# Seven block products over pairs of feature tiles for the long sequence's gate and up-projection, with the down-projection as a phase of its own

## The chip, the cores and the metric

The kernel runs on one core of one Trainium2 chip. The metric is the device time of one launch in microseconds. One launch computes the whole encoder layer for two sequences that share the weights: a long one of 1024 tokens and a short one of 512 tokens. TensorE (PE) multiplies, VectorE (DVE), ScalarE (ACT) and GpSimd (POOL) do the elementwise work, and SyncE (SP) issues all DMAs from one queue. Each engine runs its own instructions strictly in the order of the program.

## The reference, cut to what matters

Everything is fp32. After the attention part, each sequence goes through the output projection and a gated feed-forward part; the change is in the latter.

```python
def conv_glu_sublayer(x, g_ffn, w_ff_gate, w_ff_up, conv_w, conv_b, w_ff_down):
    n = rms_norm(x, g_ffn)
    gate = n @ w_ff_gate                      # 1024 -> 2816
    pad = jnp.pad(gate, ((0, 0), (1, 1), (0, 0)))
    gate = pad[:, :-2] * conv_w[0] + pad[:, 1:-1] * conv_w[1] + pad[:, 2:] * conv_w[2] + conv_b
    return x + (jax.nn.gelu(gate, approximate=False) * (n @ w_ff_up)) @ w_ff_down
# then: h = rms_norm(h, g_final); the 16 meta tokens in front are dropped
```

The convolution has width 3 over positions, so the gate at the first real token needs the gate at the last meta token too.

## The kernel before, in words

**Precision.** Each fp32 operand is split into two numbers of a type that PE reads in one pass: `hi`, the value cast on ACT (line 102), and `lo`, the rest, subtracted on DVE or POOL (line 103). A product is three matmuls into the same PSUM bank (`mm3`, lines 108 to 110): hi·hi, hi of the weights times lo of the input, lo of the weights times hi of the input.

**Layout.** Features lie on the 128 partitions, tokens along the free dimension. A weight tile (`w_f`, 128x1024, 512 KB) holds eight 128x128 blocks: the columns of one tile of output features, for all eight tiles (`KT`) of the 1024 input features. `load_weight` (lines 121 to 129) loads one and splits it.

**Order of the stages.** The program is written with generators, which `merge` interleaves. First come the two projections and the attentions. The short sequence's output projection and feed-forward part (`f1`) run beside the long sequence's attention and then beside the long sequence's output projection (`mixer_out`, line 772), which works in three chunks of 340 to 344 tokens and keeps its result `h` in SBUF. What is left of `f1` is its last group of down-projections in two halves of 256 tokens, and the final norm with its output stores (`y`, lines 635 to 644). For the short sequence there are two `y` buffers of 128x256 and one buffer for the squares that POOL adds up (line 487).

**The long sequence's feed-forward part** (`conv_glu(0)`, line 778) is the end of the program. It first scales `h` by the norm into `xhi`, `xlo` (lines 559 to 566), chunk by chunk, so that PE starts on the first chunk while the others are made. Then it goes through the 22 tiles of the 2816 features in eleven pairs. For each pair: gate products in three chunks of 342 to 344 tokens, convolution straight from PSUM (lines 585 to 589), Gelu, up products in three chunks, multiplied into the gate (line 603) and split, and then the down-projection of the two tiles at once, in 16 products of 512 tokens, each added to `h` on DVE (line 615). For the last pair the down-projection runs in four chunks of 256 tokens, and the final norm of each follows while the next is multiplied.

**What sets the order.** The framework schedules the instructions of each engine ahead of time, from the dependences, the buffers of the pools and a model of their times. The resulting order is fixed in the program.

## Time and profile before

| | us |
|---|---|
| median of 3 runs (2226.34 to 2230.16) | 2229.71 |
| profiled execution | 2230.43 |
| its span, first to last instruction | 2228.6 |
| PE busy | 2128.2 (95%) |
| DVE busy | 1463.7 (66%) |
| ACT busy | 1069.8 (48%) |
| POOL busy | 812.3 (36%) |
| granted PE clock, mean | 0.98 |

Times of the trace count from the start of the span. A timeline row gives start, duration, engine, line, operation, output <- inputs, shape, and in brackets the idle time before it with what ended it. Matmuls overlap, so the cost of one is the distance from its start to the next one's start, not its duration.

### The profile page before, as it was taken

How to read it: one execution, taken by the hardware profiler on the slowest of the kernel's cores; microseconds unless marked ns; L12 is line 12 of the kernel's file. 1: busy time of each engine (PE TensorE's matmuls, PEld its weight loads, DVE VectorE, ACT ScalarE, POOL GpSimd, SP SyncE). 2: the span in 40 equal slices, each digit the busy share in tenths (PEclk: the TensorE clock that was granted, in tenths of full speed). 3: DMA queues.
4: the chain of work that ended last, by engine and by line, in shares of the span. 5: the costliest groups of instructions: out<-in, count | busy, mean ns of one | idle time of the engine just before them, and what ended most of it. 6: DMA issues, size and time to landing. Idle time of an engine off the chain costs nothing.

```text
span 2228.6 us, 36288 instructions
## 1 busy us (share of the span) xinstructions
PE 2128.2 (95%) x13474; PEld 1984.5 (89%) x13474; DVE 1463.7 (66%) x3453; ACT 1069.8 (48%) x1921; POOL 812.3 (36%) x649
## 2 busy tenths in 40 slices
PE   7999998997999999999999999999999999999997
PEld 6888888996987998898988899989999999999997
DVE  6876787767788777788878865784443344433446
ACT  6534566544567566776776655551222221212224
POOL 3465546864445333355444423431111000111005
PEclk9999999998999999999999999999999999999999
DMA  6555335446321322232322125721111111111112
GB/s 226 163 168 191 113 93 157 166 170 196 101 80 54 101 72 65 72 124 80 121 90 76 65 73 172 221 93 48 48 38 57 48 48 48 48 38 57 48 39 76
DMA packets 113137, 219.80 MB, mean 99 GB/s; under 512 B 13728, under 2 KB 69824, under 8 KB 112448
## 3 DMA queue, kind: packets, MB, share of 16 engines
q1 hardware_dynamic: 112960, 217.48, 30.4%
q8 instruction: 106, 1.74, 0.3%
q14 instruction: 71, 0.58, 0.1%
HBM read 168.93 MB, written 48.50 MB: 98 GB/s over the span
## 4 chain that ended last, share of the span: by engine, by line
PE 76%; DVE 12%; issue 4%; ACT 4%; DMA 3%; POOL 2%; SPq 1%; DVEq 0%; ACTq 0%; POOLq 0%
PE ps_mm L108 18%; PE ps_mm L109 18%; PE ps_mm L110 18%; PE ps_t L370 5%; PE ps_s L347 3%; PE ps_s L348 3%; DVE p L349 2%; DVE w_lo L103 2%; PE ps_o L385 1%; PE ps_o L384 1%; PE ps_s L108 1%; PE ps_s L110 1%; PE ps_s L109 1%; DMA w_f<-w_in 1%; DMA x<-xT 1%
## 5 line engine op out<-in xcount | busy, mean ns | idle before, releaser
L108 PE MATMUL ps_mm<-xhi,w_hi 128*128 128x342 f32 (+6 forms) x2320 | 726.5, 314 | 12.4 <-ACT xhi L177 6.4
L109 PE MATMUL ps_mm<-xlo,w_hi 128*128 128x342 f32 (+6 forms) x2320 | 721.3, 311 | 8.8 <-DVE xlo L103 4.6
L110 PE MATMUL ps_mm<-xhi,w_lo 128*128 128x342 f32 (+6 forms) x2320 | 719.8, 310 | 0.0
L108 PEld LDWEIGHTS ps_mm<-xhi,w_hi 128*128 128x128 f32 x2320 | 441.5, 190 | 20.2 <-ACT xhi L177 7.2
L109 PEld LDWEIGHTS ps_mm<-xlo,w_hi 128*128 128x128 f32 x2320 | 441.6, 190 | 16.3 <-DVE xlo L103 6.8
L110 PEld LDWEIGHTS ps_mm<-xhi,w_lo 128*128 128x128 f32 x2320 | 442.1, 191 | 1.0
L102 ACT CAST w_hi<-w_f 128x1024 fp32r<-128x1024 f32 x200 | 207.5, 1047 | 388.9 <-PE ps_mm L109 341.9
L103 POOL TENSOR_TENSOR a_lo<-gate,a_hi 128x256 fp32r<-128x256 f32 (+2 forms) x110 | 120.4, 1097 | 725.6 <-ACT a_hi L102 725.6
L103 DVE TENSOR_TENSOR w_lo<-w_f,w_hi 128x1024 fp32r<-128x1024 f32 x183 | 264.6, 1453 | 125.9 <-ACT w_hi L102 123.8
L349 DVE TENSOR_SCALAR_CACHE_REDUCE p<-ps_s 114x344 f32<-114x344 f32 (+4 forms) x562 | 257.6, 487 | 41.8 <-PE ps_s L348 23.3
L615 DVE TENSOR_TENSOR h<-ps_mm,h 128x512 f32<-128x512 f32 (+1 forms) x288 | 182.0, 644 | 122.3 <-PE ps_mm L110 121.4
L354 ACT ACTIVATE p<-p,nm 114x1040 f32<-114x1040 f32 (+5 forms) x212 | 215.0, 1014 | 87.3 <-DVE nm L352 84.5
L102 ACT CAST pt_hi<-ps_t 128x512 fp32r<-128x512 f32 (+6 forms) x360 | 168.8, 483 | 154.4 <-PE ps_t L370 132.4
L421 POOL TENSOR_TENSOR p<-p,r 128x1040 f32<-128x1040 f32 (+1 forms) x96 | 159.2, 1666 | 188.0 <-DVE r L356 125.7
L109 PE MATMUL ps_mm<-a_lo,w_hi 128*128 128x512 f32 (+1 forms) x576 | 216.1, 375 | 2.1 <-POOL a_lo L103 2.1
L108 PE MATMUL ps_mm<-a_hi,w_hi 128*128 128x512 f32 (+1 forms) x576 | 213.8, 382 | 2.4 <-DVE h L615 1.6
L110 PE MATMUL ps_mm<-a_hi,w_lo 128*128 128x512 f32 (+1 forms) x576 | 215.7, 374 | 0.0
L103 DVE TENSOR_TENSOR pt_lo<-ps_t,pt_hi 128x512 fp32r<-128x512 f32 (+4 forms) x312 | 171.7, 561 | 50.5 <-ACT pt_hi L102 49.0
L347 PE MATMUL ps_s<-k,q 128*114 128x348 f32 (+4 forms) x552 | 184.3, 338 | 14.3 <-DVE p L349 13.7
L370 PE MATMUL ps_t<-ident,p 128*128 128x128 f32 (+7 forms) x1188 | 183.6, 270 | 2.4 <-DVE pt_lo L103 2.1
L348 PE MATMUL ps_s<-k,q 128*114 128x348 f32 (+4 forms) x552 | 172.8, 318 | 1.3 <-DMA q<-qk 1.3
L370 PEld LDWEIGHTS ps_t<-ident,p 128*128 128x128 f32 (+7 forms) x1188 | 140.9, 136 | 31.6 <-issue 6.8
(158 smaller groups left out, 3638.3 us busy)
## 6 DMA issues: line engine op xcount, KB each, us to landing
w_f<-w_gate SPq DMA_DIRECT2D x44, 512.0 KB, 3.5
w_f<-w_up SPq DMA_DIRECT2D x44, 512.0 KB, 3.5
w_f<-w_down SPq DMA_DIRECT2D x44, 512.0 KB, 3.6
w_f<-w_in SPq DMA_DIRECT2D x36, 512.0 KB, 4.1
w_f<-w_out SPq DMA_DIRECT2D x32, 512.0 KB, 3.6
q<-qk SPq DMA_DIRECT2D x32, 257.0 KB, 3.7
q<-qk SPq DMA_DIRECT2D x48, 171.0 KB, 2.9
qk<-hi SPq DMA_DIRECT2D x42, 192.0 KB, 2.0
```

The costliest lines, as they stand in the source:

```text
L102: nc.scalar.copy(hi, src)
L103: (lo_engine or nc.vector).tensor_tensor(out=lo, in0=src, in1=hi.bitcast(F32), op=ALU.subtract)
L108: nc.tensor.matmul(ps, lhsT=whi, rhs=xhi, start=start, stop=False)
L109: nc.tensor.matmul(ps, lhsT=whi, rhs=xlo, start=False, stop=False)
L110: nc.tensor.matmul(ps, lhsT=wlo, rhs=xhi, start=False, stop=stop)
L347: nc.tensor.matmul(ps, lhsT=q[0], rhs=k[:, c0:c0 + cw], start=True, stop=False)
L348: nc.tensor.matmul(ps, lhsT=q[1], rhs=k[:, c0:c0 + cw], start=False, stop=True)
L349: nc.vector.tensor_scalar(out=p[:, c0:c0 + cw], in0=ps, scalar1=HD ** -0.5, scalar2=-3.0e38, op0=ALU.mult, op1=ALU.max, accum_out=mx[:, i: ...
L354: nc.scalar.activation(p, p, AF.Exp, bias=nm, accum_out=l)
L370: nc.tensor.transpose(tps[:, c:c + M], p[:, k0:k0 + kw], g.ident[:M, :M])
L421: nc.gpsimd.tensor_tensor(out=p, in0=p, in1=r.broadcast_to([P, n]), op=ALU.mult)
L615: nc.vector.tensor_tensor(out=hs, in0=ps, in1=hs, op=ALU.add)
```

## The change

For a pair of feature tiles, the 1024 input features are cut into halves of 512 (four tiles each), and the 1024 real tokens into halves of 512. The pair's weights are then a 2x2 matrix of blocks a11, a12 (first tile), a21, a22 (second tile), the input a 2x2 matrix x11, x12, x21, x22. Eight block products would make the four results. The changed kernel makes them by seven, with sums of weight blocks (s1 to s4, on POOL, anew for each pair) and of input blocks (t1 to t4, once), and combines the products with additions (u2, v, u3). One block product is four tiles times three matmuls of 512 tokens.

- `combine` makes the seven input matrices, each as hi and lo, before the first product.
- The gate at the last meta token is made apart: eight multiply-adds on DVE over 128x128 (`g0`, lines 808 to 810) and one fp32 matmul with a vector of ones (line 813), per tile.
- `winograd` makes the seven products of a pair; weight halves of 512 columns are split with six buffers each for hi and lo (`HB`), with three buffers for whole weights (`WB`) and three for sums (`SB`).
- The products gate·up (`act`) go to DRAM. After all eleven pairs a second phase reads them back and does the down-projection for three chunks of tokens (512, 256, 256): eight PSUM banks, one for each output tile, add up over all 22 feature tiles. So `w_down` is loaded and split three times. The residual `h` is written to DRAM by `mixer_out` and read back at each chunk's end, which is followed by the final norm.

```diff
@@ mixer_out
-                w = load_weight(g, wp, g.w_out[j], bufs=wb)
+                w = load_weight(g, wp, g.w_out[j], bufs=wb) if s == 1 else load_halves(g, wp, g.w_out[j])
...
+                    if s == 0:
+                        nc.sync.dma_start(out=g.h[j, :, c0:c0 + cw], in_=h[:, j, c0:c0 + cw])
@@ new
+def split_half(g, wp, src, lo_engine=None):
+    hi = wp.tile([P, H], F32R, name="w_hi", tag="w_hi", bufs=HB)
+    lo = wp.tile([P, H], F32R, name="w_lo", tag="w_lo", bufs=HB)
+    split(g, hi, lo, src, lo_engine)
+    return hi, lo
...
+def combine(g, st, xp, tp):
...
+    def normed(k, c0):
+        hs = h[:, k, c0:c0 + H]
+        nc.vector.scalar_tensor_tensor(out=hs, in0=hs, scalar=g.gain[:, V_GFFN + k:V_GFFN + k + 1],
+                                       in1=rstd[:, c0:c0 + H], op0=ALU.mult, op1=ALU.mult)
+        return hs
+    def kept(nm, i, src):
+        split(g, x[nm][0][:, i], x[nm][1][:, i], src, nc.gpsimd if i % 2 else nc.vector)
+    def minus(a, b, i):
+        t = tp.tile([P, H], F32, name="x_t", tag="x_t", bufs=4)
+        (nc.vector if i % 2 else nc.gpsimd).tensor_tensor(out=t, in0=a, in1=b, op=ALU.subtract)
+        return t
...
+    for i in range(HT):
+        x11[i], x21[i] = normed(i, 1), normed(HT + i, 1)
+        kept("x11", i, x11[i])
+        kept("x21", i, x21[i])
+    for i in range(HT):
+        x12[i], x22[i] = normed(i, 1 + H), normed(HT + i, 1 + H)
+        t1 = minus(x12[i], x11[i], i)
...
+def winograd(g, wp, up, x, raw):
...
+    s1 = s_(ALU.add, a21, a22)
+    p1 = product(split_half(g, wp, a11), x["x11"])
+    c1 = tile("c1")
+    nc.scalar.copy(c1, p1)
+    yield 0, 0, product(split_half(g, wp, a12), x["x21"]), c1
+    p5 = product(split_half(g, wp, s1), x["t1"])
+    c5 = tile("c5")
+    nc.scalar.copy(c5, p5)
+    s2 = s_(ALU.subtract, s1, a11)
+    u2 = plus("u2", nc.vector, product(split_half(g, wp, s2), x["t2"]), c1)
+    v = plus("v", nc.gpsimd, u2, c5)
+    s3 = s_(ALU.subtract, a11, a21)
+    p7 = product(split_half(g, wp, s3), x["t3"])
+    u3 = plus("u3", nc.vector, p7, u2)
+    yield 1, 1, p7, v
+    s4 = s_(ALU.subtract, a12, s2)
+    yield 0, 1, product(split_half(g, wp, s4), x["x22"]), v
+    yield 1, 0, product(split_half(g, wp, a22), x["t4"]), u3
+def conv_glu_long(ctx, g, st, wp, es_h):
...
+        for i in range(2):
+            acc = up.tile([P, P], F32, name="g0", tag="g0")
...
+            ps = g.psum.tile(P, 2, "mm")
+            nc.tensor.matmul(ps, lhsT=acc, rhs=g.ones2, start=True, stop=True)
+            nc.scalar.copy(gate[:, i, 0:1], ps[:, 0:1])
+        for i, half, ps, rest in winograd(g, wp, up, x, raw):
+            nc.vector.tensor_tensor(out=gate[:, i, 1 + half * H:1 + (half + 1) * H], in0=ps, in1=rest, op=ALU.add)
...
+        for i, half, ps, rest in winograd(g, wp, up, x, raw):
+            a = act[:, i, half * H:(half + 1) * H]
+            t = up.tile([P, H], F32, name="sum", tag="sum")
+            nc.vector.tensor_tensor(out=t, in0=ps, in1=rest, op=ALU.add)
+            nc.gpsimd.tensor_tensor(out=a, in0=t, in1=a, op=ALU.mult)
+        for i in range(2):
+            nc.sync.dma_start(out=g.act[f0 + i], in_=act[:, i])
...
+    for c0, cw in ((0, H), (H, H // 2), (H + H // 2, H // 2)):
+        last = c0 + cw == N
+        ps = [g.psum.tile(P, cw, "mm") for _ in range(KT)]
+        for f in range(NFF):
+            a = op.tile([P, H], F32, name="a_f", tag="a_f", bufs=3)[:, :cw]
+            nc.sync.dma_start(out=a, in_=g.act[f, :, c0:c0 + cw])
+            ahi, alo = (t[:, :cw] for t in split_act(g, wp, a, cw))
+            w = load_halves(g, wp, g.w_down[f])
+            for j in range(KT):
+                mm3(g, ps[j], *block(w, j), ahi, alo, f == 0, f == NFF - 1)
...
+            nc.vector.tensor_tensor(out=h[:, j], in0=ps[j], in1=res, op=ALU.add)
...
+                sq = op.tile([P, H], F32, name="sq", tag="sq", bufs=4)[:, :cw]
+                nc.scalar.activation(sq, h[:, j], AF.Square)
+                nc.gpsimd.tensor_tensor(out=acc, in0=acc, in1=sq, op=ALU.add)
...
+            mean_rsqrt(g, op, rs, acc, cw)
@@ trunk_kernel
-    drain(conv_glu(ctx, g, 0, st0, "left", wp0, 3, 2))
+    drain(conv_glu_long(ctx, g, st0, wp0, es_h))
```

Three places of the order that the framework made, on the engines that wait or are waited for. The numbers behind the names are the program's numbers of the tiles.

PE, from the long sequence's output projection to its feed-forward part, before: `ps_s` is the last tile of the projection, `ones_d` the matmul that sums squares for the norm, `xhi` the scaled input.

```order
L108 MATMUL ps_s_16959<-xhi_16342,w_hi_16952 128x340
L109 MATMUL ps_s_16959<-xlo_16350,w_hi_16952 128x340
L110 MATMUL ps_s_16959<-xhi_16342,w_lo_16953 128x340
L492 MATMUL ps_s_17024<-acc_16358,ones_d_108 128x340
L108 MATMUL ps_mm_19035<-xhi_18916,w_hi_19031 128x344
```

The same place in the change (`a_hi` is the short sequence's activation, in its last down-projections, `g0` the gate at the last meta token):

```order
L112 MATMUL ps_s_17082<-xhi_16426,w_lo_17072 128x340
L110 MATMUL ps_mm_18932<-a_hi_18718,w_hi_18784 128x256
...
L520 MATMUL ps_s_17148<-acc_16442,ones_d_110 128x340
L520 MATMUL ps_mm_18943<-acc_18791,ones_d_110 128x256
L110 MATMUL ps_mm_18977<-a_hi_18654,w_hi_18778 128x256
...
L520 MATMUL ps_mm_18999<-acc_18878,ones_d_110 128x256
L813 MATMUL ps_mm_19193<-ones2_112,g0_19184 128x2
L813 MATMUL ps_mm_19205<-ones2_112,g0_19196 128x2
L110 MATMUL ps_mm_19214<-x11_hi_19050,w_hi_19210 128x512
```

Before, PE went from the norm's sum straight to the first gate product. Now 15 down-projection matmuls and two norm sums of the short sequence, and the two `g0` matmuls, stand between the last output projection and the first block product.

DVE at that place in the change: `y` is the short sequence's output (12 rows of it stand here, two of them shown), `x_t` a sum of input blocks.

```order
L712 SCALAR_TENSOR_TENSOR h_15044<-h_15044,gain_130,rstd_15045 128x512 x8
L645 TENSOR_TENSOR h_6876<-ps_mm_18977,h_6876 128x256
...
L671 SCALAR_TENSOR_TENSOR y_18951<-h_6876,gain_130,rstd_6877 128x256
...
L671 SCALAR_TENSOR_TENSOR y_19026<-h_6876,gain_130,rstd_6877 128x256
L707 SCALAR_TENSOR_TENSOR x0_19064<-h_15044,rstd_15045,gain_130 128x8
L105 TENSOR_TENSOR x11_lo_19051<-h_15044,x11_hi_19050 128x512
...
L721 TENSOR_TENSOR x_t_19166<-h_15044,x_t_19156 128x512
L808 TENSOR_SCALAR g0_19184<-w_f_19180,x0_19064 128x128
L808 TENSOR_SCALAR g0_19196<-w_f_19182,x0_19064 128x128
```

The short sequence's outputs, which before lay among the output projection's instructions, now all stand behind its last row; the input matrices' splits stand behind them, and `g0` behind these. On ACT the first cast of x11 likewise stands behind the last `y`.

PE at the change from the first to the second chunk of the new down phase (22855 is the last of the eight banks of the first chunk, 23819 the first of the second):

```order
L110 MATMUL ps_mm_22855<-w_hi_23698,w_hi_23708 128x512
L111 MATMUL ps_mm_22855<-w_lo_23699,w_hi_23708 128x512
L112 MATMUL ps_mm_22855<-w_hi_23698,w_lo_23709 128x512
L520 MATMUL ps_mm_23785<-acc_23738,ones_d_110 128x512
L110 MATMUL ps_mm_23819<-w_hi_23829,w_hi_23835 128x256
```

The norm's sum over the chunk that has ended stands ahead of the first product of the next one.

More of the change, by code (lines that the diff above doesn't have):

```diff
@@ L23 @@
 KT = D // P
+H = D // 2
+HT = KT // 2
 NMETA = 16
@@ L667, in merge, with split_act @@
+def split_act(g, wp, a, cw):
+    hi = wp.tile([P, H], F32R, name="w_hi", tag="w_hi", bufs=HB)
+    lo = wp.tile([P, H], F32R, name="w_lo", tag="w_lo", bufs=HB)
+    split(g, hi[:, :cw], lo[:, :cw], a)
+    return hi, lo
 def merge(a, wa, b, wb):
@@ L689 @@
 MB = 5
+HB = 6
+WB = 3
+SB = 3
 R1, R2, R3 = (1.0, 0.9), (1.0, 0.4), (1.0, 1.0)
@@ L714, in trunk_kernel @@
     nc.vector.memset(g.ones_d, 1.0 / D)
+    g.ones2 = const.tile([P, 2], F32, name="ones2")
+    nc.vector.memset(g.ones2, 1.0)
     g.ones_v = const.tile([P, P], F32, name="ones_v")
```

123 lines of the change are left out of this document (117 added, 6 removed).

## The prediction

> **What bounds the kernel now.** I read the page's engine shares first, then busy time by stretches, then the timeline of PE where the changed part begins and ends.
>
> ```profile
> span 2228.6 us, 36288 instructions
> PE 76%; DVE 12%; issue 4%; ACT 4%; DMA 3%; POOL 2%; SPq 1%; DVEq 0%; ACTq 0%; POOLq 0%
> 1440.00:1500.00 60.00, 54.97 (x322) 52.03 (x321) 49.89 (x77) 30.92 (x57) 21.64 (x21) 0.94 0.33 104
> 1600.00:1800.00 200.00, 200.00 (x1147) 188.92 (x1146) 82.77 (x119) 43.18 (x57) 20.56 (x18) 1.00 0.15 48
> L591 ACT ACTIVATE gate<-gate x11: 1913/1915/1915, 1501.6 to 2167.8; 128x2048 f32<-128x2048 f32 x11
> 1460.29 0.32 PE L110 MATMUL ps_s<-xhi,w_lo 128*128 128x340 f32 x1
> 1465.48 0.99 PE L108 MATMUL ps_mm<-xhi,w_hi 128*128 128x344 f32 x1
> 2216.43 0.28 PE L110 MATMUL ps_mm<-a_hi,w_lo 128*128 128x256 f32 x1
> ```
>
> The third and fourth rows give PE, weight loads, DVE, ACT and POOL in a stretch. From 1600 to 1800 us PE never rests, and DVE works 41% of the time. The eleven Gelus, one for each pair, are (2167.8 − 1501.6)/10 = 66.6 us apart. So the long sequence's feed-forward part, from 1465.5 to the last down product at 2216.5, is 751 us in which matmul pace alone counts.
>
> **The matmul work.** The pace of each width, from the first and the last of a run without gaps (24 of 340 to 342 tokens, 10 of 512, 12 of 256):
>
> ```profile
> 1504.24 0.32 PE L108 MATMUL ps_mm<-xhi,w_hi 128*128 128x342 f32 x1
> 1507.86 0.32 PE L110 MATMUL ps_mm<-xhi,w_lo 128*128 128x342 f32 x1
> ...
> 1518.77 0.39 PE L110 MATMUL ps_mm<-a_hi,w_lo 128*128 128x512 f32 x1
> 1520.81 0.39 PE L110 MATMUL ps_mm<-a_hi,w_lo 128*128 128x512 f32 x1
> ...
> 2210.79 0.28 PE L108 MATMUL ps_mm<-a_hi,w_hi 128*128 128x256 f32 x1
> 2212.11 0.28 PE L110 MATMUL ps_mm<-a_hi,w_lo 128*128 128x256 f32 x1
> ```
>
> That is 3.62/23 = 0.157 us, 2.04/9 = 0.227 us and 1.32/11 = 0.120 us. A pair before: 288 x 0.157 + 96 x 0.227 = 67 us, as the Gelus say. Afterwards: seven products x 12 matmuls x 2 (gate, up) x 11 pairs = 1848 of 512 tokens, 419 us; the 22 `g0` matmuls of two columns have no row, and lie between nothing and the norm's fp32 sum of 256 columns (ten records, five sums, in 2.32 us: 0.46 us); I take 0.3, being mostly weight load, 6.6 us. Down: 22 x 24 = 528 of 512 tokens, 119.7 us, and 1056 of 256, 126.7 us. Together 672 us against 751: **79 us are gained**, most of it from the eighth product, some from 512 columns in place of 342.
>
> **The seam, part one: PE waits for stores.** The changed order gives the gain back at the start. On PE the two `g0` matmuls stand ahead of the first product, and `g0` is the last thing that DVE makes, behind all input sums, which stand behind the short sequence's twelve `y` on DVE (four more on ACT and POOL). Before, PE rested here for 4 us only, since the `y` lay among the output projection and the first chunk of x was enough to start.
>
> ```profile
> 1464.68 1.50 PE L492 MATMUL ps_s<-acc,ones_d 128*128 128x340 f32 x2 [4.07 <-POOL acc L487]
> 1463.69 0.94 POOL L487 TENSOR_TENSOR acc<-acc,sq 128x340 f32<-128x340 f32 x1 [0.69 <-ACT sq L486]
> 1466.21 0.54 ACT L92 ACTIVATE rs_y<-ps_s,eps 128x340 f32<-128x340 f32 x1 [1.84 <-PE ps_s L492]
> 1470.48 0.50 DVE L96 SCALAR_TENSOR_TENSOR rstd<-rstd,rs_y 128x340 f32<-128x340 f32 x1
> L487 POOL TENSOR_TENSOR acc<-acc,sq 128x256 f32<-128x256 f32 x42 | 36.5, 870 | 29.5 <-ACT sq L486 27.7 <-ACT acc L483 0.7
> L641 DVE SCALAR_TENSOR_TENSOR y<-h,gain,rstd x12: 472/485/1146, 1415.6 to 1461.5; 128x256 f32<-128x256 f32 x12
> L443 POOL TENSOR_TENSOR p<-p,c 104x528 f32<-104x528 f32 x8 | 8.5, 1068 | 11.1 <-PE ps_mm L110 8.0 <-DVE c L441 2.6 <-PE ps_s L348 0.2
> L103 DVE TENSOR_TENSOR w_lo<-w_f,w_hi 128x1024 fp32r<-128x1024 f32 x60 | 72.8, 1228 | 60.0 <-ACT w_hi L102 60.0
> L102 ACT CAST w_hi<-w_f 128x1024 fp32r<-128x1024 f32 x60 | 62.0, 1049 | 298.8 <-PE ps_mm L109 298.8
> yT<-y SPq DMA_DIRECT2D x16, 128.0 KB, 3.0
> DVE y L641 <- DMA yT<-y: 5.3, 4, 2.6
> DMA to landing us min/median/max: 1.8/3.0/4.9
> ```
>
> I count s from the end of the last output-projection matmul, 1460.6 before; in the change 15 down matmuls (1.8 us) and two norm sums (about 1) of the short sequence come after it instead, so s = 0 at 1457.8.
> - To s = 7: square, POOL sum, norm sum, Ln, Exp, Square and the two steps on DVE (before, from 1460.6 to 1471 behind other work).
> - To s = 13: DVE scales eight tiles of 512, at about 0.8 us each (0.56 for 344 in a row of part two).
> - To s = 19: POOL adds the short sequence's squares with four input sums between; with one square buffer each add (0.87) also waits for ACT. PE then has its 12 down matmuls, and DVE the norm: first `y` at s = 22.
> - Sixteen `y` pass through two buffers. One takes about 0.5 us and lands 1.8 to 3.0 us after issue; at 2.5 a pair takes 3.05, eight pairs 24.4, less the last landing, plus 1.5 for the slower ones on ACT and POOL: the first cast of x11 at s = 45.5.
>
> **The seam, part two: the input matrices.** From there 28 casts on ACT (half of 1.05 us each) are hidden beside DVE and POOL: 22 operations of 512 on DVE, half of 1.23, so 0.6 each, 13 us; 18 on POOL at 1.05 (from the 528-wide row), 19 us. Whether these add up, two rows decide, of the same operation with and without POOL beside it:
>
> ```profile
> 1468.42 0.79 POOL L103 TENSOR_TENSOR xlo<-t,xhi 128x344 fp32r<-128x344 f32 x1 [2.07 <-ACT xhi L102]
> 1468.44 1.15 DVE L562 SCALAR_TENSOR_TENSOR t<-h,gain,rstd 128x344 f32<-128x344 f32 x1
> 1470.00 0.56 DVE L562 SCALAR_TENSOR_TENSOR t<-h,gain,rstd 128x344 f32<-128x344 f32 x1
> ```
>
> DVE's lasts 0.59 us longer, nearly POOL's whole 0.79. So I add them: 32 us, the last sum at s = 78. The three first weight sums on POOL (s1 to s3), whose splits stand between the sixteen `g0` steps on DVE, add 6: **the first product at s = 84**. Bounds: landing at 1.8 and no exclusion give 64, landing at 3.0 and POOL's slower rows 92. The Trainium skill, page "SBUF — State Buffer", section "SBUF: two separate sides", states that a DVE instruction with two SBUF inputs and a GpSimd instruction take one port pair in turn, each for its whole length; by that all 40 operations exclude each other and the seam is 84, without it 75. The quoted pair of rows agrees, and no other row here tests it on operations of 512.
>
> **Cold restarts.** After the 4 us of rest PE is slow for a while:
>
> ```profile
> 1467.24 0.49 PE L110 MATMUL ps_mm<-xhi,w_lo 128*128 128x344 f32 x1
> 1470.11 0.40 PE L108 MATMUL ps_mm<-xhi,w_hi 128*128 128x344 f32 x1
> 2208.11 0.70 PE L656 MATMUL ps_mm<-sq,ones_d 128*128 128x256 f32 x2 [2.17 <-ACT sq L655]
> ```
>
> Ten intervals take 2.87 us, 0.287 each in place of 0.157, from 1465.5 to 1470.1: a loss of 2.3 us. After the rest of 2.17 us at 2208 the next matmuls run at full pace. So a rest of 4 us costs 2.3 more, one of 2 nothing. The Trainium skill, "TensorE: Matmul & The Clock Gate", section "What's actually happening", puts both the idle window and the slow time at about 3.4 us; by it a restart would cost 1.7, and the sum below be 2 us less; the trace shows 4.6 us at half pace here.
>
> **The phases.** In the product phase a pair takes 38.7 us on PE. DVE has fourteen splits (8.7), sixteen `g0` steps (about 4), twelve additions from PSUM (0.69 each, 8.3, by the row below) and four convolution steps (about 5), 26; POOL fourteen operations, 15; ACT some 15. Splits run up to five products (13.6 us) ahead, so nothing is added; if DVE and POOL excluded each other throughout it would be 41 instead of 38.7, 25 us in all: the upper bound.
>
> ```profile
> L615 DVE TENSOR_TENSOR h<-ps_mm,h 128x512 f32<-128x512 f32 x160 | 108.7, 691 | 94.7 <-PE ps_mm L110 94.7
> w_f<-w_down SPq DMA_DIRECT2D x44, 512.0 KB, 3.6
> 2195.35 4.01 POOL L487 TENSOR_TENSOR acc<-acc,sq 128x256 f32<-128x256 f32 x5 [0.16 <-ACT sq L486]
> 2216.55 2.32 PE L656 MATMUL ps_mm<-sq,ones_d 128*128 128x256 f32 x10
> ```
>
> - Into the down phase: the store of the last activation stands ahead of the loads of the first ones on SP. Addition, POOL product, store, load (about 3), cast and split against one product left on PE: 3 us of rest (0 to 6).
> - In the 256-token chunks a step is 24 x 0.12 = 2.9 us, against 1.7 us of DVE, 1.6 of ACT and 0.64 MB loaded with three buffers at 3.6 us. That fits, barely: 0, at most 0.4 x 44 = 18.
> - At a chunk's end the norm's sum stands ahead of the next product on PE. It waits for seven POOL additions, 1.07 each at 512 wide (the first 2.5 us before the end, so until 5.0 after) and 0.8 at 256 (until 5.2). With the sums and a cold restart each: 8.3 + 8.1 = 16.4 us. The final norm's steps on DVE then delay the next splits, about 3 (0 to 8).
> - The end: before, 12.1 us from the last down product; eight norm sums instead of five follow it, 3 x 0.46 more: 13.4.
> - The stores of `h` and the halved splits in the output projection are hidden by PE, which waits there for nothing; uncovered, a few us.
>
> **Sum.** 1457.8 + 84 + 2.3 + (419 + 6.6) + 3 + 246.4 + 16.4 + 3 + 13.4 = 2251.9 us, 23 above the span. The profiled execution is 1.8 longer than its span and 0.7 above the median: **2253 us, 1.0% slower**.
>
> **The rivals.**
> - *The seam is short: `y` does not hold up its successors, and DVE and POOL work side by side.* Then s = 22 + 9 + 23 + 6 = 60, and the time 2229, no slower; from s = 56 down it is faster by itself, and with rests of 5 us at the chunks' ends it is 2222. For it: DVE is idle for more than half of the time from 1600 to 1800. Against it: `y` waits for landings before too (four times, up to 2.6 us), and s would be below my lower bound. Chance 0.16.
> - *DVE sets the pace* in the product phase (POOL's exclusion) or in the 256-token chunks: 10 to 43 us more, 2263 to 2296. For it: 41 against 38.7 by sums. Against it: five products of lead. 0.2.
> - *The change does not do what it says.* Excluded by its order: 84 matmuls of 512 stand there for each pair's gate, where eight products of 12 would be 96. Chance 0.
>
> **How the numbers follow.** 0.64 for my case, 2235 to 2265 by its own bounds. The range takes in the second rival's lower half and the edge of the first: 2230 to 2282. About 0.2% (4.5 us) can be told from no change. Faster: most of the first rival, 0.11. Same: its rest and a little of mine, 0.08. Slower: 0.81.
>
> **What would show it.** Right: a rest of 70 to 90 us on PE ended by `g0` at about 1460 to 1540, with `y` waiting for its DMA ahead of it; 512-wide matmuls 0.227 apart and pairs 38 to 40 us apart; two rests of 5 to 7 us ended by POOL's `acc`, followed by a few us of slow matmuls. Wrong: a seam under 60 us, pairs more than 40 us apart, or a down phase whose 256-token steps take over 3 us.

## The result: 3.3% slower, by a chain of waits and by slower matmuls

| | before | changed kernel |
|---|---|---|
| time, median (range), us | 2228.89 (2226.34 to 2230.16) | 2303.47 (2295.91 to 2304.31) |
| span of the profiled execution, us | 2228.6 | 2302.5 |
| ratio | | 1.0329, 95% interval 1.0305 to 1.0352 |
| forecast | | 2253 (2230 to 2282) |

The sign was right and the size was not: 50.6 us of span are missing in the prediction (2302.5 against 2251.9). The page's first row of the changed kernel, and its chain of waits:

```profile
span 2302.5 us, 36074 instructions
...
PE 18%; DVE 7%; DMA 5%; POOL 4%; issue 3%; ACT 1%; SPq 0%; POOLq 0%; ACTq 0%; DVEq 0%
```

In the kernel before, PE held 76% of that chain. Now it holds 18%, and the rest passes from engine to engine. The busy time by stretches (PE, weight loads, DVE, ACT, POOL, then the clock and the DMA share): the seam, 200 us of products, the first chunk of the down phase.

```profile
1460.00:1545.00 85.00, 6.43 (x18) 3.94 (x17) 58.53 (x69) 30.23 (x61) 53.10 (x44) 0.50 0.07 25
1600.00:1800.00 200.00, 192.21 (x826) 153.37 (x825) 151.36 (x220) 67.38 (x107) 93.27 (x63) 1.00 0.20 69
2015.00:2136.00 121.00, 121.00 (x527) 100.06 (x528) 47.86 (x74) 41.78 (x72) 1.18 (x1) 0.99 0.48 160
```

PE is no longer always busy among the products, DVE works 76% of that time and not 41%, and the down phase is as full as was forecast. The places where PE stood, from its timeline:

```profile
1456.05 0.32 PE L112 MATMUL ps_s<-xhi,w_lo 128*128 128x340 f32 x1
...
1478.92 1.22 PE L520 MATMUL ps_mm<-acc,ones_d 128*128 128x256 f32 x2 [17.86 <-POOL acc L515]
...
1489.70 1.22 PE L520 MATMUL ps_mm<-acc,ones_d 128*128 128x256 f32 x2 [6.11 <-POOL acc L515]
1545.22 1.01 PE L813 MATMUL ps_mm<-ones,g 128*128 128x2 f32 x4 [54.30 <-DVE g L810]
1546.09 0.77 PE L110 MATMUL ps_mm<-x_hi,w_hi 128*128 128x512 f32 x1
...
1706.16 0.50 PE L112 MATMUL ps_mm<-t_hi,w_lo 128*128 128x512 f32 x1 [1.19 <-DVE w_lo L105]
...
1710.57 0.39 PE L110 MATMUL ps_mm<-x_hi,w_hi 128*128 128x512 f32 x1
...
1715.25 0.40 PE L112 MATMUL ps_mm<-x_hi,w_lo 128*128 128x512 f32 x1
...
2136.16 0.39 PE L112 MATMUL ps_mm<-w_hi,w_lo 128*128 128x512 f32 x1
2144.96 2.08 PE L520 MATMUL ps_mm<-acc,ones_d 128*128 128x512 f32 x2 [8.41 <-POOL acc L875]
```

The first product comes at 1546.1, 4.3 us later than forecast. From 1710.57 to 1715.25 lie 20 intervals: 0.234 us for a matmul of 512 columns, where 0.227 was taken from the down-projection. At 1706 a split of weights is late. In the table, measured terms are worked out from the starts of the matmuls in the trace (rounded, so their sum is 0.3 above the span):

| term of the sum | forecast, us | measured, us |
|---|---|---|
| first product at | 1541.8 | 1546.1 |
| cold restart behind the seam | 2.3 | 2.2 (first pair 42.0, the next two 39.8) |
| 1848 matmuls of the products | 419 | 433 (0.2343 each) |
| `g0` matmuls | 6.6 | 4.4 (0.44 a pair: 39.8 less 168 x 0.2343) |
| stalls in the products | 0 | 24.5 (the last seven of ten intervals between pairs: 42.1 to 44.2) |
| into the down phase | 3 | 4.8 |
| down phase with chunk ends and restarts | 246.4 + 16.4 + 3 | 121.4 + 9.7 + 66.8 + 8.5 + 66.1 = 272.5 |
| end | 13.4 | 15.3 |

Of the 50.6 us that are missing, 24.5 are the stalls, 14 the pace of the products' matmuls, 6.7 the down phase with its chunk ends and 4.3 the seam; smaller terms make up the rest.

**The stalls are a closed chain of waits.** The second and the third pair take 39.8 us, the later ones some 43.3. One turn of that chain, from the timelines of DVE, POOL, ACT and SP (SPq is SP's queue of DMA issues; the second number is the duration or the issue's wait):

```profile
1680.16 1.30 POOL L837 TENSOR_TENSOR act<-sum,act 128x512 f32<-128x512 f32 x1
1678.98 2.83 SPq L839 DMA_DIRECT2D act<-act  x2
1681.92 11.42 SPq L138 DMA_DIRECT2D w_f<-w_gate  x2
1685.90 0.28 DVE L808 TENSOR_SCALAR g<-w_f,x 128x128 f32<-128x128 f32 x1 [8.09 <-DMA w_f<-w_gate]
1689.29 0.69 DVE L766 TENSOR_TENSOR u<-ps_mm,c 128x512 f32<-128x512 f32 x1
1690.12 1.61 POOL L766 TENSOR_TENSOR v<-u,c 128x512 f32<-128x512 f32 x1 [7.41 <-DVE u L766]
1691.76 0.69 DVE L816 TENSOR_TENSOR gate<-ps_mm,v 128x512 f32<-128x512 f32 x1 [0.59 <-POOL v L766]
1694.17 1.25 ACT L822 ACTIVATE act<-gate,vec 128x1024 f32<-128x1024 f32 x1 [8.86 <-DVE gate L816]
1699.08 1.27 DVE L823 SCALAR_TENSOR_TENSOR act<-gate,vec,act 128x1024 f32<-128x1024 f32 x1
1706.30 1.27 DVE L825 SCALAR_TENSOR_TENSOR act<-gate,vec,act 128x1023 f32<-128x1023 f32 x1
1707.60 1.92 ACT L827 ACTIVATE act<-act 128x2048 f32<-128x2048 f32 x1 [3.60 <-DVE act L825]
1709.60 1.29 POOL L837 TENSOR_TENSOR act<-sum,act 128x512 f32<-128x512 f32 x1 [5.43 <-ACT act L827]
1723.02 1.28 POOL L837 TENSOR_TENSOR act<-sum,act 128x512 f32<-128x512 f32 x1
1721.38 3.27 SPq L839 DMA_DIRECT2D act<-act  x2
1724.76 0.37 SPq L138 DMA_DIRECT2D w_f<-w_gate  x1
```

SP issues in order. The next pair's gate weights stand behind the store of the previous pair's activations, and that store waits for POOL's last multiplication. DVE's order has the next pair's `g0` steps ahead of the running pair's additions `u`, so DVE stands still for 8.1 us with work behind it. When the weights are there, the additions, `v` on POOL, the convolution, Gelu and POOL's four multiplications follow one another, and the last of them releases the next store: 1681.92 to 1724.76, 42.8 us a turn. These rows are the main links and not all: the profile's own chain through this turn also passes through the loads of the second gate tile and of an up tile (3.2 and 3.1 us), each behind a weight sum on POOL, and puts 2.4 us on PE.

### The profile page after: what moved, and what is told of

Read it like the earlier page. It is cut to its first block, busy times and chain, and to the rows that moved or that the text cites. A ratio compares the mean times of both kernels' runs of the same rounds, so it can differ in the third digit from the quotient of the medians.

```text
span 2302.5 us, 36074 instructions
## 1 busy us (share of the span) xinstructions
PE 2082.9 (90%) x12628; PEld 1861.9 (81%) x12628; DVE 1657.9 (72%) x3745; ACT 1182.8 (51%) x2178; POOL 976.9 (42%) x738
## 5 line engine op out<-in xcount | busy, mean ns | idle before, releaser
L105 DVE TENSOR_TENSOR w_lo<-w_f,w_hi 128x512 fp32r<-128x512 f32 (+1 forms) x339 | 343.5, 1031 | 157.4 <-ACT w_hi L104 156.9
L110 PE MATMUL ps_mm<-xhi,w_hi 128*128 128x258 f32 (+3 forms) x1264 | 389.7, 309 | 12.3 <-ACT xhi L205 6.8
L111 PE MATMUL ps_mm<-xlo,w_hi 128*128 128x258 f32 (+3 forms) x1264 | 383.4, 303 | 9.1 <-DVE xlo L105 3.4
L112 PE MATMUL ps_mm<-xhi,w_lo 128*128 128x258 f32 (+3 forms) x1264 | 381.0, 301 | 0.0
L104 ACT CAST w_hi<-w_f 128x512 fp32r<-128x512 f32 (+1 forms) x356 | 259.9, 750 | 210.6 <-PE ps_mm L111 152.8
L382 ACT ACTIVATE p<-p,nm 114x1040 f32<-114x1040 f32 (+5 forms) x212 | 215.0, 1014 | 91.6 <-DVE nm L380 88.9
L110 PEld LDWEIGHTS ps_mm<-xhi,w_hi 128*128 128x128 f32 x1264 | 242.2, 192 | 19.1 <-ACT xhi L205 7.4
L111 PEld LDWEIGHTS ps_mm<-xlo,w_hi 128*128 128x128 f32 x1264 | 242.0, 191 | 15.5 <-DVE xlo L105 5.4
L112 PEld LDWEIGHTS ps_mm<-xhi,w_lo 128*128 128x128 f32 x1264 | 242.1, 192 | 1.0
L375 PE MATMUL ps_s<-k,q 128*114 128x348 f32 (+4 forms) x552 | 184.1, 338 | 15.1 <-DVE p L377 13.6
L110 PE MATMUL ps_mm<-w_hi 128*128 128x256 f32 (+1 forms) x528 | 163.1, 325 | 6.4 <-ACT w_hi L104 6.4
L111 PE MATMUL ps_mm<-w_lo,w_hi 128*128 128x256 f32 (+1 forms) x528 | 161.4, 323 | 0.0
```

The costliest lines, as they stand in the source:

```text
L104: nc.scalar.copy(hi, src)
L105: (lo_engine or nc.vector).tensor_tensor(out=lo, in0=src, in1=hi.bitcast(F32), op=ALU.subtract)
L110: nc.tensor.matmul(ps, lhsT=whi, rhs=xhi, start=start, stop=False)
L111: nc.tensor.matmul(ps, lhsT=whi, rhs=xlo, start=False, stop=False)
L112: nc.tensor.matmul(ps, lhsT=wlo, rhs=xhi, start=False, stop=stop)
L375: nc.tensor.matmul(ps, lhsT=q[0], rhs=k[:, c0:c0 + cw], start=True, stop=False)
```

## The experiments

Two theories stood against each other for the products. A: that closed chain. B: DVE's work, some 33 us of each pair as it ran with POOL beside it (76% of 43.3), sets the pace (the prediction's second rival). The end of the output projection, which none of the edits touches, lies between 1446 and 1460 us in these profiles, which alone moves a single time by several us, so phases are compared:

| kernel | seam | products | behind | time, us |
|---|---|---|---|---|
| changed kernel | 90.0 | 463.8 | 292.6 | 2304.3 |
| act_store_pool | 89.0 | 438.9 | 286.2 | 2270.0 |
| g0_late | 46.0 | 470.8 | 292.6 | 2264.3 |
| g0_none | 47.8 | 464.3 | 291.1 | 2260.1 |
| sums_pe | 88.9 | 461.8 | 285.2 | 2291.6 |
| seam_dve | 76.7 | 460.5 | 290.3 | 2283.6 |
| y_buffers | 82.1 | 461.7 | 290.5 | 2288.2 |
| short_sums_pe | 79.2 | 460.4 | 289.8 | 2279.0 |
| two_banks | 90.2 | 439.8 | 288.4 | 2273.3 |
| five_with_g0 | 22.9 | 465.2 | 279.6 | 2221.6 |
| five_without_g0 | 58.5 | 439.8 | 279.2 | 2234.0 |
| five_x_moved_96 | 23.1 | 452.1 | 279.7 | 2210.1 |

The seam is counted from the last matmul of the output projection to the first product, the products to their last matmul. Where `g0` stands behind, PE starts early and then waits among the first products (their first pair takes 66 to 73 us), so there the sum of both counts. The phases are those of the profiled execution, the time is the median where there were several. In kernels whose edit leaves a phase alone it differs by up to 1.3 us (seam) or about 3 us (products, behind). All seven edits that were first made to the changed kernel came out faster than expected of them, by up to 14 us; 1 to 8 us of that is the end of the output projection, which was late, at 1456.2, in the profile that the expectations started from.

### The store on another queue

```
-            nc.sync.dma_start(out=g.act[f0 + i], in_=act[:, i])
+            nc.gpsimd.dma_start(out=g.act[f0 + i], in_=act[:, i])
```

> Edit: the two stores of the finished activations of a pair are issued by POOL, right behind its own multiplication, and no longer by SP, where they stand ahead of the next pair's gate weights. The order on DVE stays the same. Theory A (a closed chain of waits: store behind POOL's multiplication, gate weights behind the store on SP, DVE's g0 behind the weights, the additions of the running pair behind g0, Gelu and POOL's multiplications behind these): the weights start some 6 us earlier, DVE's wait for them falls from 81 us in nine pairs to under 25, pairs fall from 43.3 us to 40 to 41, and the time to 2280 to 2288 us. Theory B (DVE's 31 us of work per pair, stretched by POOL, set the pace): nothing about that work changes, pairs stay at 42.5 to 43.5 and the time at 2300 to 2306.

Every pair but the first takes 39.8 us, and the time is 2270.0. The waits from 1600 to 1900 us, of the changed kernel (us in total, times, longest):

```profile
DVE g L808 <- DMA w_f<-w_gate: 58.3, 13, 8.4
PE ps_mm L112 <- DVE w_lo L105: 10.1, 9, 1.2
```

and of this one, with its busy time in the same stretch:

```profile
DVE g L808 <- DMA w_f<-w_gate: 14.8, 14, 2.2
```

```profile
1600.00:1900.00 300.00, 300.00 (x1297) 241.80 (x1296) 257.70 (x346) 111.46 (x174) 157.29 (x117) 1.00 0.22 78
```

DVE does more in that time, 86% busy with POOL at 52% beside it, and PE never rests. Theory B falls: DVE had the room. The products take 24.9 us less, which is all of the stalls. Behind them another 6.4 us are gone, of which only the 4.8 of the rest at the phase change stand clear of the 3 us by which this phase varies: the first matmul of the down phase now follows the last product by 0.24 us, because the first loads of activations no longer stand behind the last store.

The Trainium skill, "DMA: Bandwidth & Descriptors", section "Issuing engines are not separate DMA queues", says that issuing from several engines saves only the sequencer's time of issue, usually little beside the transfer. Here the transfers hardly changed (512 KB each, a store landing in 3.0 us and not 2.8, gate weights in 3.2 and not 3.3), and the other queue saved some 30 us in these two stretches, since on SP an issue that waited for its data held up the issues behind it.

### The place of g0

The sixteen steps and two matmuls go behind the gate products' loop:

```
-        for i in range(2):
-            acc = up.tile([P, P], F32, name="g0", tag="g0")
...
-            nc.scalar.copy(gate[:, i, 0:1], ps[:, 0:1])
         for i, half, ps, rest in winograd(g, wp, up, x, raw):
             nc.vector.tensor_tensor(out=gate[:, i, 1 + half * H:1 + (half + 1) * H], in0=ps, in1=rest, op=ALU.add)
+        for i in range(2):
+            acc = up.tile([P, P], F32, name="g0", tag="g0")
...
+            nc.scalar.copy(gate[:, i, 0:1], ps[:, 0:1])
```

> Edit: the sixteen g0 steps on DVE and the two g0 matmuls come behind the seven gate products of the same pair, not ahead of them. Theory A (the closed chain through DVE's wait for the gate weights): DVE no longer stands still for the weights with the running pair's additions behind it; pairs 40 to 41 us from about 43.3, time 2275 to 2290; the seam loses the g0 steps too (about 10 us less, the first product at about 1535). Theory B (DVE's work, stretched by POOL): the same work in another order, pairs stay at 42.5 or more; only the seam's 10 us are won, 2293.

Pairs of 39.8 us again, with the store still on SP, and from 1600 to 1900 us PE never rests:

```profile
1600.00:1900.00 300.00, 300.00 (x1297) 241.79 (x1296) 246.77 (x353) 113.63 (x173) 164.19 (x107) 1.00 0.23 80
```

The chain is broken at its other link. Seam and products together are 516.8 us against 553.8, 37 less: 24.5 of stalls, and 12.5 at the seam. Leaving the steps out altogether, so that a copied column stands where the gate at the last meta token should be:

```
-        for i in range(2):
-            acc = up.tile([P, P], F32, name="g0", tag="g0")
...
-            nc.scalar.copy(gate[:, i, 0:1], ps[:, 0:1])
+        for i in range(2):
+            nc.scalar.copy(gate[:, i, 0:1], g.x0[:, 0:1])
```

> Left out: the gate of the one token before the sequence (sixteen steps on DVE, two matmuls per pair); a copy of one column stands in its place, so the output of the first token is another one. Theory A: no DVE wait for weights ahead of the additions, pairs at the matmul work, 168 x 0.234 = 39.3 us; time 2262 to 2275 with 10 us less in the seam. Theory B: DVE's work falls by some 9 us of 31 per pair, so pairs also fall to 39.3; the run tells the theories apart only by DVE's idle time: under A DVE was idle beforehand too (11 us of each pair) and idles some 18 now. For the pace of one matmul, 0.234 us in place of the 0.227 of the prediction: if it comes from DVE's and POOL's traffic it falls with it, if from the form of the products it stays at 0.234.

```profile
1600.00:1900.00 300.00, 300.00 (x1282) 241.15 (x1281) 190.42 (x228) 113.26 (x175) 164.81 (x107) 1.00 0.23 83
```

Pairs take 39.4 us. DVE's 8 us of `g0` per pair cost nothing as work, only by their place. And with DVE at 63% the matmul still takes 0.2343 us: its pace is not a matter of DVE's traffic.

### The seam

```
-        split(g, x[nm][0][:, i], x[nm][1][:, i], src, nc.gpsimd if i % 2 else nc.vector)
+        split(g, x[nm][0][:, i], x[nm][1][:, i], src, nc.vector)
...
-        (nc.vector if i % 2 else nc.gpsimd).tensor_tensor(out=t, in0=a, in1=b, op=ALU.subtract)
+        nc.vector.tensor_tensor(out=t, in0=a, in1=b, op=ALU.subtract)
```

> Edit to the changed kernel: all 40 elementwise operations of the seven input matrices on DVE, none of the 18 on POOL. If a DVE operation and a POOL operation on these tiles take turns (the prediction's reading: 22 x 0.6 + 18 x 1.05 = 32 us add up), POOL's 18 now cost 0.6 us each in place of 1.07: from the first cast to the last sum 24 to 25 us in place of 30, the first product 5 to 8 us earlier, time 2295 to 2299. If the two engines work side by side, DVE's 40 operations in line take longer than 22 did, and the seam grows by 5 to 10 us: 2308 to 2314.

The groups of DVE and POOL instructions in the seam, of the changed kernel (us busy, mean ns):

```profile
L105 DVE TENSOR_TENSOR t_lo<-x_t,t_hi 128x512 fp32r<-128x512 f32 x8 | 10.5, 1334 | 1.8 <-ACT t_hi L104 1.8
L105 POOL TENSOR_TENSOR t_lo<-x_t,t_hi 128x512 fp32r<-128x512 f32 x8 | 12.4, 1566 | 3.8 <-ACT t_hi L104 3.8
```

and of the edited one:

```profile
L105 DVE TENSOR_TENSOR t_lo<-x_t,t_hi 128x512 fp32r<-128x512 f32 x16 | 10.4, 676 | 0.0
```

DVE makes all sixteen in the time that eight took with POOL beside. The seam is 13.3 us shorter, more than expected, but not where it was expected: from the first cast to the last sum it is 28.0 us in place of 30.4 (24 to 25 were expected). The eight scalings ahead take 7.1 us in place of 10.7 and the `g0` steps behind 7 in place of 12, being freed of POOL as well. The prediction's reading that the two engines take turns on these tiles holds for the single operations. The Trainium skill, "SBUF — State Buffer", section "SBUF: two separate sides", says so of a DVE instruction with two SBUF inputs; the trace agrees (676 ns against 1334). What taking turns cost here lay mostly outside the input matrices.

```
-                y = op.tile([P, ob, cw], F32, name="y", tag="y", bufs=2 if s == 1 else 4) if k % ob == 0 else y
+                y = op.tile([P, ob, cw], F32, name="y", tag="y", bufs=8 if s == 1 else 4) if k % ob == 0 else y
```

> Edit to the changed kernel: eight buffers in place of two for the short sequence's output tiles y. The prediction has the sixteen y wait for their own stores, 23 us from the first y to the first cast of the input matrices. If so, DVE's 8.8 us and ACT's 10.3 us of waiting for these stores go, and the first cast comes 5 to 12 us earlier: 2291 to 2298. If the second chunk's norm holds the last y anyway, only the six y behind it come closer together: 3 to 5 us, 2298 to 2300.

```profile
1478.18 4.70 DVE L671 SCALAR_TENSOR_TENSOR y<-h,gain,rstd 128x256 f32<-128x256 f32 x6
...
1487.82 0.49 DVE L97 SCALAR_TENSOR_TENSOR rstd<-ps_mm,eps,rstd 128x256 f32<-128x256 f32 x1 [4.60 <-ACT rstd L96]
...
1488.80 5.74 DVE L671 SCALAR_TENSOR_TENSOR y<-h,gain,rstd 128x256 f32<-128x256 f32 x6
```

In this timeline of DVE six `y` run together. Then the second chunk's norm is late, and six more follow. The seam is 7.9 us shorter: the stores cost about that much, and 4.6 us of the rest was the norm's.

```
-            sums = s == 0 and c0 + cw == N
-            acc = g.psum.tile(P, cw, "mm") if sums else op.tile([P, cw], F32, name="acc", tag="acc", bufs=ob)
+            sums = True
+            acc = g.psum.tile(P, cw, "t") if sums else op.tile([P, cw], F32, name="acc", tag="acc", bufs=ob)
```

> Edit to the changed kernel: the short sequence's sums of squares (its last step, at the seam) by sixteen fp32 sums on PE, not by additions on POOL with one buffer for the squares. If POOL's chain of additions holds the first y (the prediction: POOL's chain to s = 19, measured 21 to 22), the two waits of PE for acc, 17.9 and 6 us, fall, the first y comes 5 to 10 us earlier and so does the first product: 2293 to 2298. If DVE's eight scalings of 512 columns (13 us with POOL beside) hold the seam, 0 to 3 us: 2300 to 2303.

The seam is 79.2 us, 10.8 less, and the time 2279.0; part of that is an output projection that ended 8 us earlier in this execution, which its edit does not explain for certain. The seam is counted from that end, so the 10.8 us do not contain it. PE's two waits for `acc` (17.9 and 6.1 us in the changed kernel) are gone.

### The chunk ends

```
-            if last:
+            if True:
                 if j == 0:
                     acc = g.psum.tile(P, cw, "mm")
...
-        if last:
+        if True:
             rsqrt_newton(g, op, rs, acc, cw)
```

> Edit: the sums of squares of the first two token chunks are made on PE from all eight squares, as in the last chunk, and no longer by seven additions on POOL. If POOL's chain of additions sets the two rests (8.8 and 7.9 us until the norm's sum), these fall to 2 to 3 us each, while eight fp32 sums of 0.9 and 0.46 us each come onto PE; 6 to 12 us less, 2292 to 2297 us. If the rests are set by the additions to h on DVE or by the loads of the residual, they stay at 7 us or more and the time rises to about 2306.

Behind the products 285.2 us in place of 292.6. PE's timeline at the end of the first chunk (an fp32 sum stands as two records):

```profile
2131.36 0.40 PE L112 MATMUL ps_mm<-w_hi,w_lo 128*128 128x512 f32 x1
2131.59 1.02 PE L869 MATMUL ps_mm<-sq,ones_d 128*128 128x512 f32 x2
2132.68 0.28 PE L112 MATMUL ps_mm<-w_hi,w_lo 128*128 128x256 f32 x1
```

The rest of 8.8 us is gone: the next chunk's matmuls run between the sums. POOL's chain did set the rests. The gain is smaller than the two rests, since PE now makes sixteen fp32 sums itself.

### The pace of a matmul

The products' matmuls took 0.2343 us and the down phase's 0.2267, at a granted clock of 1.00 and 0.99 (the down phase's first 4 us are a restart). With the store on POOL, two products at a time, so that the PSUM bank changes every three matmuls:

```
-    p1 = product(split_half(g, wp, a11), x["x11"])
+    p1, q = two(split_half(g, wp, a11), x["x11"], split_half(g, wp, a12), x["x21"])
...
+        for i in range(HT):
+            mm3(g, ps[0], *block(a, i), b[0][:, i], b[1][:, i], i == 0, i == HT - 1)
+            mm3(g, ps[1], *block(c, i), d[0][:, i], d[1][:, i], i == 0, i == HT - 1)
```

> Edit to the kernel with the activation stores on POOL (2268.2 us span): the seven products of a block are made two at a time, three matmuls into one PSUM bank, then three into the other, as the down-projection changes bank after three; the seventh as before. Disputed: why a matmul of 512 columns takes 0.234 us in the products and 0.227 in the down phase, at the same granted clock. If long runs of matmuls into one bank are slow: 0.227 in six of seven products, 1584 x 0.0075 = 12 us less, pairs of 38.7 us, time about 2258. If it is the moving operand, which changes with every feature block here and stays for eight blocks in the down phase: 0.234 as before, and pairs of 39.8 us or somewhat more, since results come out later: 2268 to 2275.

0.2343 as before: not the bank. Next, on the kernel with all edits (its own section follows), the down phase's moving operand in the pool that takes over the memory of the input matrices:

```
-            ahi, alo = (t[:, :cw] for t in split_act(g, wp, a, cw))
+            ahi, alo = (t[:, :cw] for t in split_act(g, op, a, cw))
```

> As the first of these three, and the split activations of the down phase (the moving operand) lie in the pool that takes the memory of the seven input matrices, not among the split weights. Disputed: a matmul of 512 columns at 0.234 us in the products, 0.227 in the down phase; changing the PSUM bank every three matmuls left it at 0.234. If the place of the moving operand beside the weights' decides, the first token chunk's matmuls go from 0.227 to 0.234 (528 x 0.0075 = 4 us more). If not, they stay at 0.227 and the time within 2 us of the first.

```profile
1989.93 0.39 PE L110 MATMUL ps_mm<-a_hi,w_hi 128*128 128x512 f32 x1
...
1995.78 0.39 PE L111 MATMUL ps_mm<-a_lo,w_hi 128*128 128x512 f32 x1
```

25 intervals in 5.85 us: 0.234 in the down phase too, and the time is 2225.6 us. So it goes with where the operand lies. In the compiled programs the input matrices begin at byte 20864 of each partition, a multiple of 128, and so did the moved operand; the fast ones begin 480 bytes behind a multiple of 512. Moving the matrices:

```
+    xp.tile([P, n], F32, name="pad")
+    g.x0 = xp.tile([P, KT], F32, name="x0")
     x = {nm: [xp.tile([P, HT, H], F32R, name=f"{nm}_{part}") for part in ("hi", "lo")] for nm in names}
-    g.x0 = xp.tile([P, KT], F32, name="x0")
```

without a pad (32 bytes), on the changed kernel and on the one with all edits, and with pads of 8, 16 and 48 columns (64, 96 and 224 bytes):

> Edit to the changed kernel: the eight columns of x0 (32 bytes in each partition) are allocated ahead of the seven input matrices, not behind them, so that all matrices lie 32 bytes further; every engine's order stays the same. Disputed: the 0.234 us of a product's matmul of 512 columns against 0.227 in the down phase. In the products the moving operand begins at a multiple of 64 bytes, in the down phase 32 bytes behind one, as the weights do in both; moving the down phase's operand to a multiple of 64 made it 0.234 there too. If the start decides: 0.227 in the products, the pairs without a stall 38.5 us in place of 39.8, the stalls of the later pairs grow (the chain of waits still takes 43 us), time 2296 to 2304. If it is the memory region: 0.234 as before and 2300 to 2305.

> The same edit on top of the five edits with g0 behind the gate products (2221.6 us), where the pairs have no stall. If the start decides, 1848 x 0.0075 = 14 us less: 2206 to 2210, 0.8 to 0.9% below the kernel before. If the region decides, 2219 to 2224.

> The seven input matrices 64 bytes further than in the first version with all edits (a pad and x0 ahead of them), nothing else. So far a product's matmul of 512 columns took 0.2343 us with its operand at a multiple of 128 bytes, 0.2333 us 32 bytes behind one; in the down phase, where the operand starts 96 bytes behind one, 0.2267. If the start within 128 bytes decides, 64 lies between or with the slow ones: 0.227 to 0.2333, time 2206 to 2220. If another property of the place decides, 0.2333 to 0.2343.

> As the last, 96 bytes further: the operand starts 96 bytes behind a multiple of 128, as in the down phase. If the start within 128 bytes decides: 0.2267 and pairs of 38.5 us, 14 us less than at multiples of 128: 2205 to 2211. If not: 0.233 to 0.234 and 2216 to 2222.

> The kernel of the run with the matrices moved by 64 bytes once more, since that run had a granted clock of 0.75 from its start to its end and tells nothing of the pace. If the pace changes step by step with the start, it lies between 0.2333 (32) and 0.2270 (96); if only one start in 128 bytes is fast, 0.233 to 0.2345; the time 2206 to 2222.

> The matrices moved by 224 bytes: again 96 bytes behind a multiple of 128, but 96 and no longer 480 behind a multiple of 512. If the start within 128 bytes decides, 0.2270 as with 96, and 2207 to 2216; if the start within 512 (or 256) decides, 0.233 to 0.234 and 2216 to 2222.

| moved by | start, modulo 128 / 512 | a matmul, us | a pair, us | time, us |
|---|---|---|---|---|
| 0 | 0 / 384 | 0.2343 | 39.8 | 2221.6 |
| 32 | 32 / 416 | 0.2333 | 39.6 | 2217.9 |
| 64 (again) | 64 / 448 | 0.2333 | 39.6 | 2212.9 |
| 96 | 96 / 480 | 0.2270 | 38.6 | 2210.1 |
| 224 | 96 / 96 | 0.2324 | 39.5 | 2219.4 |

The times for 64 and 224 bytes are single executions. On the changed kernel itself, 32 bytes gave 0.2333 too, and 2295.8 us. The first run with 64 bytes (2565.3 us) was granted a clock of 0.75 from start to end, so its pace cannot be compared. Ahead is the kernel with all edits unmoved, 26 intervals:

```profile
1649.78 0.39 PE L110 MATMUL ps_mm<-t_hi,w_hi 128*128 128x512 f32 x1
...
1655.87 0.40 PE L112 MATMUL ps_mm<-x_hi,w_lo 128*128 128x512 f32 x1
```

and moved by 96 bytes, 27 intervals in about the same time:

```profile
1649.73 0.39 PE L112 MATMUL ps_mm<-x_hi,w_lo 128*128 128x512 f32 x1
...
1655.85 0.39 PE L112 MATMUL ps_mm<-t_hi,w_lo 128*128 128x512 f32 x1
```

The place of the moving operand decides, neither the bank nor the engines beside PE. The period is not 128 bytes, since 224 gave 0.2324; 256 or 512 would fit, and which of them, and why, stays open. One rival is untested: in the compiled programs the split weights of the long sequence also start 480 bytes behind a multiple of 512, in every run, so wherever a matmul was fast its two operands started alike, and no run separates the start itself from the start relative to the weights.

The profile of the kernel before had a slow stream already, the short sequence's down products, whose operand starts 64 bytes and whose weights start 352 bytes behind a multiple of 512:

```profile
1315.04 0.39 PE L109 MATMUL ps_mm<-a_lo,w_hi 128*128 128x512 f32 x1
...
1317.38 0.40 PE L110 MATMUL ps_mm<-a_hi,w_lo 128*128 128x512 f32 x1
```

10 intervals in 2.34 us, 0.234, at a granted clock of 1.00.

### All edits together

The five edits that had each shortened a part (store on POOL, sums on PE in the down phase and in the short sequence, input matrices on DVE, eight `y` buffers), with and without the later place of `g0`:

> All edits that shortened a part of the changed kernel, together: activation stores on POOL, g0 behind the gate products, sums of squares on PE in the down phase and in the short sequence's last step, all input-matrix operations on DVE, eight y buffers. If each takes away its own wait, the parts add up from the span of 2302.5: store 31 (25 in the product phase, 6 at the phase change and behind), g0 16, sums 7, DVE 13, y 8, short sums 11: 2216 us, 2208 to 2222, below the kernel before (about 2229). If they sit in the same rests (y, short sums and g0 all in front of one first product), the smaller ones vanish: 2225 to 2240, no gain on the kernel before.

> The same without moving g0: the g0 steps stay ahead of the gate products. Parts that add up: 2232 us (2224 to 2238), so that the place of g0 is worth about 16 us; if DVE's steps for g0 are hidden once POOL is idle in the seam, the difference falls to under 8 us.

With `g0` behind: 2221.55 us, ratio 0.9972 (0.9960 to 0.9984), a little faster than the kernel before. The span of 2216.9 is what the expectation added up from the single edits (85.6 us less than 2302.5), in part by luck: the phases themselves are 78.7 us shorter, and the other 6.8 us are an output projection that ended earlier in this execution. Without `g0` behind, the time is 2234.0; in seam and products together the place of `g0` is worth 10.2 us there. With the matrices moved by 32 bytes the ratio is 0.9949 (0.9931 to 0.9967). **With 96 bytes it is 2210.1 us, ratio 0.9909 (0.9892 to 0.9926)**: with its waits and its pace mended, the changed program is the faster one. How much of that the seven products earn is not shown, since the kernel before was given none of these edits and its operands were not moved. PE still waits some 28 us in the first pair, 18 of them for the cast of a weight sum, which stands on ACT behind the last cast of the input matrices.

## Why the prediction was right and wrong

- **Matmul work: right in count, wrong in one duration.** 0.227 was read from the down-projection and used for the products, which took 0.2343: 433 us in place of 419. The width was the same, the place of the operand was not. The short sequence's down products in the same trace, at 0.234, would have shown that 512 columns have more than one price.
- **The seam: right in its path, in its size partly by luck.** 84 us from 1457.8 were forecast, 88 were measured (90 from the projection's actual end, 1456.2). From DVE's and ACT's timelines:

```profile
1483.18 1.41 DVE L671 SCALAR_TENSOR_TENSOR y<-h,gain,rstd 128x256 f32<-128x256 f32 x2
1503.02 1.12 ACT L104 CAST x_hi<-h 128x512 fp32r<-128x512 f32 x2
1531.64 1.75 DVE L721 TENSOR_TENSOR x_t<-h,x_t 128x512 f32<-128x512 f32 x1
1533.31 2.50 DVE L808 TENSOR_SCALAR g<-w_f,x 128x128 f32<-128x128 f32 x2
```

The first `y` came at s = 25.4 (forecast 22), the first cast of x11 at 45.2 (45.5), the end of the last sum at 75.6 (78). So the stores' stretch took 19.8 us for 23.5 and the input matrices 30.4 for 32.5, which partly made up for a first `y` that came 3.4 late and for the `g0` steps, which took 12 us, not 6, with POOL's weight sums beside them. That DVE and POOL take turns, the run with all operations on DVE confirmed; the prediction has 9 us rest on it, though by its own rows (32 us added up, against POOL's 19 alone) it would be 13.
- **"Splits run up to five products (13.6 us) ahead, so nothing is added": the step that failed.** Throughput was right in its outcome: PE's work exceeds DVE's, and with the store elsewhere PE never rests, although DVE is then busy for 34 us of a pair (86% of 39.8) and not 26. But the order was not followed round. `g0` was counted as 4 us of work on DVE, and the wait in front of it, for weights that stand on SP behind a store that waits for the previous pair, has no term. It cost 24.5 us, more than any other error, and without it the time would have been some 2279 us, inside the forecast range. The second rival named the price (10 to 43 us) with another cause, POOL's exclusion; that cause fell.
- **Into the down phase: 4.8 for 3.** The reason was right, and the store's other queue took the rest away. The restart behind it (eight matmuls 0.43 us apart, 1.7 us lost) was not counted.
- **Chunk ends: right in cause, mis-sized.** POOL's additions at the two ends:

```profile
2134.82 10.09 POOL L875 TENSOR_TENSOR acc<-acc,sq 128x512 f32<-128x512 f32 x7 [122.36 <-ACT sq L874]
...
2213.97 0.72 POOL L875 TENSOR_TENSOR acc<-acc,sq 128x256 f32<-128x256 f32 x1 [52.25 <-ACT sq L874]
```

At 512 wide one took 1.44 us and not 1.07, and the first began 1.6 us ahead of the chunk's end, not 2.5; at 256 wide the first came 1.2 us behind the end (2212.8). So the norm's sums waited 8.8 and 7.9 us, not 5. With the restarts the ends cost 24 us in place of 19.4, a stall of 2 us in the second chunk among them.
- **256-token chunks: right.** Their matmuls go at 0.12 us, and but for that stall PE waits for nothing there.
- **The end: 15.3 for 13.4**, by the same steps.
- **The restart behind the seam: right**, 2.2 us for 2.3.

## What to carry to other kernels

Where every engine and the DMA queue run in a fixed order, a throughput sum per engine is not enough: follow one period round, from the load that a step waits for, to what stands ahead of that load on its queue, to what that waits for, and see whether it returns to the step. A store that waits for its data belongs on a queue where nothing urgent stands behind it, and a step that waits for a load belongs behind the work that is ready. Before a block product is judged by its saved matmuls, price the operand sums at its start, where nothing hides them.

## What was not expected of the hardware

A matmul of 512 columns took 0.2270 us where its moving operand starts 480 bytes behind a multiple of 512 in the partition, as its weights do, and 0.2324 to 0.2343 us at the other four starts tried: 3%, or 13 us over 1848 matmuls, for 96 bytes of padding. Nearly all of its single intervals are 0.226 and 0.227 in the first case; they spread from 0.228 to 0.241 in the others. The Trainium skill, "TensorE: Matmul & The Clock Gate", section "Back-to-back issue gap", gives about 0.216 us as the gap of an isolated 512-column matmul at full clock; no run here came to that value.
